# A two-layer hybrid encoder trunk: softmax division after the product with v, and head pairs prepared one step earlier

## The chip, the cores and the metric

The kernel runs on one core of a Trainium2 chip. The time is the device time of one execution, in microseconds; for the kernel before it is 1597.09 us, the median of three runs (1595.65 to 1597.92).

## The reference

Two layers over one sequence of 512 tokens with 1024 features, in float32. Each layer has a mixing part and a feed-forward part.

```python
h = modulate(rms_norm(x, norm_mix[i]), sh1, sc1)      # sh1.. g2 = c_act @ w_ada[i] + b_ada[i], six vectors of 1024
# hybrid_mixer: one projection of h is split among three mixers
o_ssm = s5_mixer(u, ...)                               # 16 groups of a diagonal state-space recurrence
o_mla = block_sweep(q, k, v_mla, ..., chunk_causal)    # 6 heads, low-rank q and kv, rotary part
o_fox = block_sweep(fqh, fkh, fvh, ..., frame_causal, log_decay=cum_log_f)   # 6 heads, forgetting bias
x = x + g1 * (concat(rms_norm of each) @ w_out)
h = modulate(rms_norm(x, norm_ffn[i]), sh2, sc2)
x = x + g2 * (swiglu(h) if i == 0 else moe_ffn(h))     # dense in layer 0, top 2 of 8 experts in layer 1

# block_sweep: 128-query blocks, each reads the keys up to its end
s = einsum(q[q0:q1], k[:q1]) * scale (+ log_decay terms), masked
p = softmax(s);  out = p @ v[:q1]
```

## The kernel before

Features lie on partitions and tokens on the free axis for most stages. A weight block is loaded by the sync engine's DMA queue (`wload`, L375), rounded by ScalarE to its high half (L382) and reduced by VectorE to its low half (L383); each product of the large matrices is then three matmuls (L399 to L401).

**Attention.** The twelve heads of a layer go in six pairs: F0, F1, F2 (the forgetting heads) and M0, M1, M2 (the low-rank heads). A pair is first prepared, by `fox_unit` or `mla_unit`: projections into PSUM, norms of q and k, and four transposes per token block into the tile `U` (three buffers), which ScalarE copies out of PSUM (L961). The low-rank units start with the matmuls L1012 and L1014 in the PSUM banks `C` (two of them); all the units' transposes (`turn`) use the banks `C` as well, and so does `mla_low`, which comes before them. `attend` then does the pair: for each head and each 128-query block i, `att_prob` computes the scores in a bank `A` (L866) and adds the mask (L867), VectorE takes the row maximum (L870), ScalarE the exponential with its row sum (L871), VectorE the reciprocal of the sum (L872), and GpSimd or VectorE multiplies the row block by it (L873). One block later `att_out` transposes the i+1 blocks of 128x128 (L882), ScalarE copies them out (L885), and they go one by one into products with v (L887): 10 products of 128 columns per head, each of which is two instructions in float32. A head writes 64 of the 128 partitions of the output bank, and the two heads of a pair come one after the other. At the pair's end ScalarE copies the bank out (L890).

**What else runs there.** The state-space mixer's parts (`s5_part`, whose products at L821 write the two halves of the partitions by turns); `s5_out`; the merges (three norms over a mixer's output); and the output projection `w`, whose tile `xs` has the buffers of the attention rows `pr`. In layer 0 there are also the rows of the modulation vectors (`ada_part`): one row is a 512 KB DMA into a tile with one buffer and a multiply-and-sum of 1.2 us on VectorE (L477); 40 rows belong to layer 0, row by row, and 24 of them lie in this stage: rows 16 to 24 give g1 for the output projection, 26 to 39 give the shift and scale that the feed-forward norm needs (L527, L516).

**What sets the order.** The string `SEQ` lists the steps of each layer: `f` and `m` prepare a unit, `A` attends the oldest prepared one, `s` is a part of the state-space mixer, `o` its output, `a,j0,j1` are modulation rows, `g` a merge, `w` a block of the output projection. The framework plans every engine's instructions from it, the earlier step first where two are ready, so steps overlap; each engine then runs its own list in order. The rows of a step `a` carry one more edge: on VectorE they come behind the last instruction of the unit prepared last ahead of them in `SEQ` (`held`, with `self.mark` set at L982 and L1045).

Of the kernel before, what the change touches and what calls it, by code (L numbers as in the profile page):

```python
# [53 lines left out]
def _most_blocks():  # L54
# [49 lines left out]
SEQ = ("""k,BBAD v,BD f,0,B p,0,4,1 f,1,A p,4,4,0 R l s,0 A s,1 m,0 A a,16,25 s,2 f,2,C A s,3 a,25,26 A o m,1 A m,2 a,26,34 g,F,A g,5,D a,34,40 A w,0,C g,M,A w,1,C w,2,C w,3,C w,4,C w,5,A w,6,C w,7,D""",
       """k,AACC R f,0,B s,0 s,1 v,A l f,1,C s,2 m,0 A A f,2,B s,3 A m,1 A o m,2 A g,F,C g,5,C A g,M,B w,0,A w,1,C w,2,B w,3,C w,4,C w,5,C w,6,C w,7,C""")
# [180 lines left out]
class Net:  # L286
# [538 lines left out]
    def s5_out(self, l, yj, pool):  # L825

        nc = self.nc
        v = nc.vector
        TT = v.tensor_tensor
        wg = pool.tile([P, 2, 256], FT, tag="sA", name="wg", bufs=1)  # L830
        nc.gpsimd.dma_start(out=wg, in_=self.a["wglu"][l].rearrange("p (k m) -> p k m", k=2))
        yT = pool.tile([P, 2, L], FT, tag="yT", name="yT", bufs=1)
        for th in range(2):
            ps = self.bank("D")
            for t in range(4):
                nc.tensor.transpose(ps[:, t * P:(t + 1) * P], yj[:, th * 4 + t].rearrange("p q c -> p (q c)"),
                                    self.C("ident"))
            for g in range(2):
                nc.scalar.copy(
                    yT[:, g].rearrange("p (j t) -> p t j", t=T8)[:, th * 4:th * 4 + 4, :],  # L840
                    ps.rearrange("p (t g j) -> p t g j", t=4, g=2)[:, :, g, :])

        gt = pool.tile([P, 2, L], FT, tag="yj", name="gt", bufs=1)
        nc.scalar.activation(gt, yT, AF.Square, scale=math.sqrt(0.044715))
        v.scalar_tensor_tensor(out=gt, in0=gt, scalar=1.0, in1=yT, op0=OP.add, op1=OP.mult)
        self.sigmoid(gt, 2.0 * math.sqrt(2.0 / math.pi))
        TT(out=yT, in0=yT, in1=gt, op=OP.mult)
        oT = pool.tile([P, 2, L], FT, tag="o5", name="o5", bufs=1)
        for m in range(2):
            ps = self.bank("D")  # L850
            for k in range(2):
                nc.tensor.matmul(ps, wg[:, k, m * P:(m + 1) * P], yT[:, k], start=(k == 0), stop=(k == 1))
            nc.scalar.activation(oT[:, m], ps, AF.Identity, bias=self.S(l, "bglu")[:, m:m + 1])
        self.sigmoid(oT, 1.0)
        TT(out=oT, in0=oT, in1=yT, op=OP.mult)
        self.dump(f"ossm{l}", oT)
        return oT

    def att_prob(self, un, hh, i, pool):

        nc, sp = self.nc, self.sp
# [4 lines left out]
        nc.tensor.matmul(ps[:, :n], U[0:r, 2 + hh, i * P:n], U[0:r, hh, 0:n], start=True, stop=False)  # L866
        nc.tensor.matmul(ps[:, n - P:n], self.identB, self.mskB[:, un["mask"]], start=False, stop=True)  # L867
        ms = sp.tile([P, 2], FT, tag="ms", name="ms")
        pr = pool.tile([P, L], FT, tag="pr", name="pr", bufs=NPR)
        v.reduce_max(out=ms[:, 0:1], in_=ps[:, :n], axis=AX.X, negate=True)  # L870
        nc.scalar.activation(pr[:, :n], ps[:, :n], AF.Exp, bias=ms[:, 0:1], accum_out=ms[:, 1:2])  # L871
        v.reciprocal(ms[:, 1:2], ms[:, 1:2])  # L872
        (nc.gpsimd if (hh * NT + i) % 8 in PRP else v).tensor_scalar(pr[:, :n], pr[:, :n], ms[:, 1:2], None, op0=OP.mult)  # L873
        return pr

    def att_out(self, un, hh, i, pr, po, pool, oT):

        nc = self.nc
        ps = self.bank("B")
        n = (i + 1) * P  # L880
        for j in range(i + 1):
            nc.tensor.transpose(ps[:, j * P:(j + 1) * P], pr[:, j * P:(j + 1) * P], self.C("ident"))  # L882
        PT = pool.tile([P, L], FT, tag="PT", name="PT", bufs=NPT)
        eng = nc.scalar.copy if (hh * NT + i) % 8 in PTA else nc.vector.tensor_copy
        eng(PT[:, :n], ps[:, :n])  # L885
        for j in range(i + 1):
            nc.tensor.matmul(po[hh * 64:hh * 64 + 64, i * P:n], un["v"][:, j, un["vo"] + hh, :],  # L887
                             PT[:, j * P:(j + 1) * P], start=(j == 0), stop=(j == i))
# [100 lines left out]
    def mla_unit(self, l, u, c, keep, pool, far):  # L989
        nc, sp = self.nc, self.sp  # L990
        v = nc.vector
        TT = v.tensor_tensor
        U = keep.tile([P, 4, L], FT, tag="U", name="U", bufs=NU)
# [14 lines left out]
        for i in range(NT):  # L1008
            tk = slice(i * P, (i + 1) * P)
            ps = self.bank("C")  # L1010
            for k in range(2):
                nc.tensor.matmul(ps[:, :192], cT[:, k, tk], wq[:, k], start=(k == 0),  # L1012
                                 stop=(k == 1))
# [3 lines left out]
                                 scale=rkv[:, i:i + 1])  # L1017
# [16 lines left out]
        qb = far.tile([P, NT, 2, 32], FT, tag="qb", name="qb", bufs=1)  # L1034
# [43 lines left out]
    def mla_low(self, l, h, kf, pool, far):  # L1078

        nc, a = self.nc, self.a  # L1080
        v = nc.vector
        TT = v.tensor_tensor
# [36 lines left out]
        kr2 = far.tile([P, NT, 32], FT, tag="kr2", name="kr2", bufs=1)  # L1119
# [21 lines left out]
    def layer_mix(self, l, xsrc, x, xst):  # L1141

        nc, tc, a = self.nc, self.tc, self.a
        v = nc.vector
        with ExitStack() as st:
            e = st.enter_context
            big = e(tc.tile_pool(name=f"big{l}", bufs=2))
            h = [big.tile([P, KD, L], FR, tag="big", name=f"h{i}") for i in range(2)]
            st3 = e(ExitStack())
            ps = self.norm_sum(x, (0, 2, 4, 6)) if l == 0 else None  # L1150
# [755 lines left out]
```

## Time and profile before

| | |
|---|---|
| profiled execution | 1599.44 us, span 1597.8 us, granted TensorE clock 0.962 |
| busy TensorE, weight loads | 1488.4 us (93%), 1236.8 us (77%) |
| busy VectorE, ScalarE, GpSimd | 1127.7 us (71%), 799.3 us (50%), 207.5 us (13%) |
| attention of layer 0 | about 98 to 300 us of the span, its output projection to 350 us, feed-forward from 357 us |
| attention of layer 1 | about 795 to 966 us |

Times are microseconds from the start of the span. A busy time of TensorE includes matmuls that only overlap in its pipeline, so 93% isn't 93% of its peak. A row of a group ends, after the bar, with the idle time of the engine just before its instructions and what ended it; a row of a timeline gives start, duration and, in brackets, idle time before it and its releaser.

### The profile page before, as it was taken

The numbers are of one execution on the slowest core, as the hardware profiler recorded it, in microseconds if no ns is written. First come the engines' busy times: TensorE is split into PE (matmuls) and PEld (weight loads), VectorE is DVE, ScalarE is ACT, GpSimd is POOL, SyncE is SP. The second block draws the span as 40 slices with busy tenths as digits, with TensorE's granted clock in tenths as the row PEclk, the third lists the DMA queues.
The fourth block names the chain that finished last, engine by engine and source line by source line (L and its number), as shares of the span: only waits on it lengthen the run. The fifth ranks groups of instructions, "written<-read, shape, count | busy, mean of one in ns | idle before, by whom it ended". The sixth has DMA issues, their size and how long they took to land.

```text
span 1597.8 us, 24585 instructions
## 1 busy us (share of the span) xinstructions
PE 1488.4 (93%) x8427; PEld 1236.8 (77%) x8427; DVE 1127.7 (71%) x2636; ACT 799.3 (50%) x1547; POOL 207.5 (13%) x286
## 2 busy tenths in 40 slices
PE   6889899889999999999999999679999999999896
PEld 5877666558888888887988666578878998898894
DVE  8695678866855577555555665778777878878885
ACT  4344357544332233233445863357556766776672
POOL 1213131102000000003322220110000001002002
PEclk7988989999999999999999999789999999999998
DMA  9323440584566657552431006378777878889885
GB/s 357 138 92 123 118 139 34 178 301 132 188 200 191 219 180 230 178 181 82 148 93 54 1 8 201 102 257 284 248 264 284 293 250 306 314 265 319 293 296 190
DMA packets 94722, 308.88 MB, mean 193 GB/s; under 512 B 12144, under 2 KB 12592, under 8 KB 94592
## 3 DMA queue, kind: packets, MB, share of 16 engines
q1 hardware_dynamic: 74880, 253.42, 46.8%
q0 software_dynamic: 12800, 41.26, 7.7%
q10 hardware_dynamic: 6912, 12.59, 2.4%
q8 instruction: 68, 1.11, 0.3%
q14 instruction: 62, 0.51, 0.1%
HBM read 283.43 MB, written 23.79 MB: 192 GB/s over the span
## 4 chain that ended last, share of the span: by engine, by line
PE 62%; DMA 12%; DVE 10%; issue 10%; ACT 3%; POOL 2%; ACTq 0%; DVEq 0%; SPq 0%; POOLq 0%
PE psB L400 4%; PE psB L401 4%; PE psB L399 4%; PE psC L400 4%; PE psC L401 4%; PE psC L399 4%; PE psB L887 3%; DMA adw<-in_wada_dram 3%; PE psA L399 3%; PE psA L401 3%; PE psA L400 3%; PE psA L866 3%; PE psB L1424 2%; PE psB L882 2%; DVE wl L383 2%
## 5 line engine op out<-in xcount | busy, mean ns | idle before, releaser
L382 ACT CAST wh<-wr 128x1024 fp32r<-128x1024 f32 (+4 forms) x402 | 395.3, 992 | 422.8 <-PE psB L400 98.3
L383 DVE TENSOR_TENSOR wl<-wr,wh 128x1024 fp32r<-128x1024 f32 (+4 forms) x402 | 458.5, 1149 | 153.0 <-ACT wh L382 149.0
L477 DVE SCALAR_TENSOR_TENSOR adw<-adw,cact 128x1024 f32<-128x1024 f32 x80 | 97.8, 1223 | 80.1 <-DMA adw<-in_wada_dram 79.9
L866 PE MATMUL psA<-U 65*128 65x128 f32 (+3 forms) x192 | 73.8, 472 | 9.8 <-DVE xn L980 7.6
L1424 PE MATMUL psB<-hgB,wh 128*128 128x432 f32 (+3 forms) x256 | 80.3, 323 | 0.5 <-ACT wh L382 0.5
L870 DVE TENSOR_REDUCE ms<-psA 128x1 f32<-128x128 f32 (+1 forms) x96 | 46.5, 487 | 42.3 <-PE psA L867 41.8
L1426 PE MATMUL psB<-hgB,wl 128*128 128x256 f32 x256 | 71.2, 283 | 0.9 <-DVE wl L383 0.9
L873 POOL TENSOR_SCALAR pr<-pr,ms 128x128 f32<-128x128 f32 (+1 forms) x48 | 49.1, 1024 | 148.6 <-DVE ms L872 100.6
L399 PE MATMUL psB<-fh,wh 128*128 128x512 f32 (+1 forms) x156 | 61.2, 392 | 4.7 <-ACT fh L517 4.7
L1424 PE MATMUL psC<-hgB,wh 128*128 128x432 f32 (+3 forms) x192 | 61.2, 324 | 2.2 <-ACT wh L382 2.0
L400 PE MATMUL psB<-fh,wh 128*128 128x512 f32 (+1 forms) x156 | 61.0, 391 | 1.0 <-POOL fh L520 0.6
L885 ACT COPY PT<-psB 128x128 f32<-128x128 f32 (+1 forms) x96 | 41.4, 436 | 38.7 <-PE psB L882 38.4
L401 PE MATMUL psB<-fh,wl 128*128 128x512 f32 (+1 forms) x156 | 60.6, 388 | 0.0
L1504 POOL DMA_DIRECT2D yd<-yt x21 | 11.8, 563 | 375.4 <-ACT yt L1494 265.7
L871 ACT ACTIVATE pr<-psA,ms 128x128 f32<-128x128 f32 (+1 forms) x96 | 51.6, 539 | 17.2 <-DVE ms L870 14.2
L1424 PE MATMUL psA<-hgB,wh 128*128 128x432 f32 (+3 forms) x184 | 58.7, 325 | 0.1
L1426 PE MATMUL psC<-hgB,wl 128*128 128x256 f32 x192 | 54.0, 284 | 2.7 <-DVE wl L383 2.7
L1426 PE MATMUL psA<-hgB,wl 128*128 128x256 f32 x184 | 51.8, 283 | 0.0
L1424 PEld LDWEIGHTS psB<-hgB,wh 128*128 128x128 f32 x256 | 48.3, 189 | 2.5 <-ACT wh L382 1.7
L1426 PEld LDWEIGHTS psB<-hgB,wl 128*128 128x128 f32 x256 | 48.3, 189 | 1.7 <-DVE wl L383 1.2
L866 PEld LDWEIGHTS psA<-U 65*128 65x128 f32 (+1 forms) x192 | 31.8, 204 | 17.5 <-issue 11.6
L882 PE MATMUL psB<-cst,pr 128*128 128x128 f32 x240 | 43.8, 292 | 0.5 <-POOL pr L873 0.5
(766 smaller groups left out, 4394.8 us busy)
## 6 DMA issues: line engine op xcount, KB each, us to landing
wr<-in_mw_dram SPq DMA_DIRECT2D x158, 512.0 KB, 4.6
adw<-in_wada_dram SPq DMA_DIRECT2D x80, 512.0 KB, 3.7
wr<-in_md_dram SPq DMA_DIRECT2D x80, 512.0 KB, 4.4
wr<-in_fg_dram SPq DMA_DIRECT2D x22, 512.0 KB, 4.3
wr<-in_fu_dram SPq DMA_DIRECT2D x22, 512.0 KB, 4.1
wr<-in_me_dram SPq DMA_DIRECT2D x16, 512.0 KB, 4.4
wr<-in_w_f_dram SPq DMA_DIRECT2D x12, 512.0 KB, 3.6
wr<-in_fd_dram SPq DMA_DIRECT2D x16, 384.0 KB, 3.2
```

The lines of the kernel that those rows point to most:

```text
L382: nc.scalar.copy(hi[:, :n], raw[:, :n])
L383: nc.vector.tensor_tensor(out=lo[:, :n], in0=raw[:, :n], in1=hi[:, :n], op=OP.subtract)
L399: mm(ps, a[0], b[0], start=start, stop=False, skip_group_check=shared)
L400: mm(ps, a[0], b[1], start=False, stop=False, skip_group_check=shared)
L401: mm(ps, a[1], b[0], start=False, stop=stop, skip_group_check=shared)
L477: nc.vector.scalar_tensor_tensor(out=w, in0=w, scalar=1.0, in1=self.cact, op0=OP.mult, op1=OP.mult, accum_out=self.ada[l][:, j:j + 1])
L866: nc.tensor.matmul(ps[:, :n], U[0:r, 2 + hh, i * P:n], U[0:r, hh, 0:n], start=True, stop=False)
L871: nc.scalar.activation(pr[:, :n], ps[:, :n], AF.Exp, bias=ms[:, 0:1], accum_out=ms[:, 1:2])
L873: (nc.gpsimd if (hh * NT + i) % 8 in PRP else v).tensor_scalar(pr[:, :n], pr[:, :n], ms[:, 1:2], None, op0=OP.mult)
L882: nc.tensor.transpose(ps[:, j * P:(j + 1) * P], pr[:, j * P:(j + 1) * P], self.C("ident"))
L1424: mm(ps[:, :2 * C], hi[:, s], h2, start=(kk == 0), stop=False, skip_group_check=True)
L1426: mm(ps[:, C:C + 2 * P], lo[:, s], h2[:, 0:2 * P], start=False, stop=(kk == KD - 1), skip_group_check=True)
```

## The change

The softmax rows are no longer divided before they are transposed. The row sums of both heads are kept, one reciprocal of the 128x8 sums is taken at the pair's end, and small products spread it over the 64 partitions of each head; VectorE multiplies the pair's output by it as it takes it out of PSUM. A head's ten 128x128 blocks are handled in three parts (`TQ`) of 3, 3 and 4 blocks instead of four; the transposed blocks of a whole head are kept (`PT0`, `PT1`), and the products with v come at the pair's end, four per head of 512, 384, 256 and 128 columns, with the two heads by turns. In `SEQ` both layers prepare a unit one attention earlier; the rows `a,16,25` of layer 0 move from behind `m,0` to behind `m,2`; in layer 1 the projection of F2 moves from the banks `B` to `C`. Some tiles change place: `xs` takes the buffers of the state-space parts, `qb`, `kr2` and the spread sums take the common 2 KB tiles, and `yT` becomes two tiles.

```diff
-SEQ = ("""k,BBAD v,BD f,0,B p,0,4,1 f,1,A p,4,4,0 R l s,0 A s,1 m,0 A a,16,25 s,2 f,2,C A s,3 a,25,26 A o m,1 A m,2 a,26,34 g,F,A g,5,D a,34,40 A w,0,C g,M,A w,1,C ...""",
-       """k,AACC R f,0,B s,0 s,1 v,A l f,1,C s,2 m,0 A A f,2,B s,3 A m,1 A o m,2 A g,F,C g,5,C A g,M,B w,0,A ...""")
+SEQ = ("""k,BBAD v,BD f,0,B p,0,4,1 f,1,A p,4,4,0 R l m,0 A s,0 f,2,C A s,1 m,1 A s,2 m,2 a,16,25 A s,3 a,25,26 A o a,26,34 g,F,A g,5,D a,34,40 A w,0,C g,M,A w,1,C ...""",
+       """k,AACC R f,0,B s,0 s,1 v,A l f,1,C s,2 m,0 A f,2,C A s,3 m,1 A m,2 A o A g,F,C g,5,C A g,M,B w,0,A ...""")
+TQ = (((0, 0), (1, 1), (0, 1)), ((2, 2), (0, 2), (1, 2)), ((0, 3), (2, 3), (3, 3), (1, 3)))
+PTO = ((0, 2), (1, 4), (3, 4), (8, 1))
...
-        v.reciprocal(ms[:, 1:2], ms[:, 1:2])
-        (nc.gpsimd if (hh * NT + i) % 8 in PRP else v).tensor_scalar(pr[:, :n], pr[:, :n], ms[:, 1:2], None, op0=OP.mult)
...
+    def att_turn(self, t, pr, at, PT):
+        ps = self.bank("B")
+        for c, (j, i) in enumerate(TQ[t]):
+            o = at[i] + j * P
+            nc.tensor.transpose(ps[:, c * P:(c + 1) * P], pr[:, o:o + P], self.C("ident"))
+        nc.scalar.copy(PT[:, o:o + n], ps[:, :n * P].rearrange("p (a b) -> p a b", a=n))
+
+    def att_out(self, un, PTs, ls, pool, oT):
+        v.reciprocal(ls, ls)
+        ps = self.bank("B")
+        for i in range(NT):
+            for hh in range(2):
+                nc.tensor.matmul(ps[hh * 64:hh * 64 + 64, i * P:(i + 1) * P],
+                                 ls[:, hh, i:i + 1].to_broadcast([P, HD]), self.C("ident"), start=True, stop=True)
+        rl = pool.tile([P, L], FT, tag="t2k", name="rl")
+        nc.scalar.copy(rl, ps)
+        po = self.bank("B")
+        for j in range(NT):
+            o, d = PTO[j]
+            for hh, PT in ((1, PTs[1]), (0, PTs[0])):
+                nc.tensor.matmul(po[hh * 64:hh * 64 + 64, j * P:], un["v"][:, j, un["vo"] + hh, :],
+                                 PT[:, o:o + (NT - 1 - j) * d + 1:d], start=(j == 0), stop=(j == NT - 1),
+                                 skip_group_check=True)
+        v.tensor_tensor(out=oT[:, un["u"], :], in0=po, in1=rl, op=OP.mult)
...
-                    xt = pool.tile([P, L], FT, tag="pr", name="xs", bufs=NPR)
+                    xt = env["far"].tile([P, L], FT, tag="s" + "ABC"[d % 3], name="xs", bufs=1)
```

## Rows read from the trace of the kernel before

**Rows 1.** The page: chain of work that ended last, shares of the span by engine.
```profile
PE 62%; DMA 12%; DVE 10%; issue 10%; ACT 3%; POOL 2%; ACTq 0%; DVEq 0%; SPq 0%; POOLq 0%
```

**Rows 2.** Matmuls, layer 0: start, us, engine, line, operation, tiles, shape, count.
```profile
226.24 0.44 PE L821 MATMUL psD<-sA,sX 128*64 128x128 f32 x4
...
227.16 0.39 PE L821 MATMUL psD<-sB,sU 128*64 128x128 f32 x4
227.39 1.04 PE L887 MATMUL psB<-PT,vm 128*64 128x128 f32 x8
228.35 0.33 PE L882 MATMUL psB<-cst,pr 128*128 128x128 f32 x1
228.52 1.02 PE L866 MATMUL psA<-U 65*128 65x512 f32 x2
229.38 0.22 PE L867 MATMUL psA<-mskB,identB 128*128 128x128 bf16 x1
```

**Rows 3.** Groups by line, layer 1 (756 to 985 us): busy, mean ns | idle.
```profile
L873 POOL TENSOR_SCALAR pr<-pr,ms 128x128 f32<-128x128 f32 (+1 forms) x24 | 24.6, 1023 | 72.1 <-DVE ms L872 49.5 <-DVE uss L1025 10.5 <-DVE kq L1043 7.1
...
L873 DVE TENSOR_SCALAR pr<-pr,ms 128x256 f32<-128x256 f32 (+1 forms) x24 | 10.2, 424 | 1.2
...
L872 DVE RECIPROCAL ms<-ms 128x1 f32<-128x1 f32 x48 | 7.6, 159 | 12.6 <-ACT pr L871 12.3
```

**Rows 4.** ScalarE's timeline, layer 1: the pair outputs of F1 and M2.
```profile
884.03 0.58 ACT L890 COPY oF<-psB 128x512 f32<-128x512 f32 x1
...
965.73 0.59 ACT L890 COPY oM<-psB 128x512 f32<-128x512 f32 x1 [2.05 <-PE psB L887]
```

**Rows 5.** VectorE's timeline, layer 0: modulation rows and units' last instructions.
```profile
177.24 1.22 DVE L477 SCALAR_TENSOR_TENSOR adw<-adw,cact 128x1024 f32<-128x1024 f32 x1
...
183.04 1.23 DVE L477 SCALAR_TENSOR_TENSOR adw<-adw,cact 128x1024 f32<-128x1024 f32 x1 [3.04 <-DMA adw<-in_wada_dram]
...
225.19 1.22 DVE L477 SCALAR_TENSOR_TENSOR adw<-adw,cact 128x1024 f32<-128x1024 f32 x1
...
267.75 0.62 DVE L1045 TENSOR_TENSOR kq<-qr,urr 128x192 f32<-128x192 f32 x2
268.29 1.22 DVE L477 SCALAR_TENSOR_TENSOR adw<-adw,cact 128x1024 f32<-128x1024 f32 x1
...
298.55 1.23 DVE L477 SCALAR_TENSOR_TENSOR adw<-adw,cact 128x1024 f32<-128x1024 f32 x1 [0.42 <-DMA adw<-in_wada_dram]
```

**Rows 6.** VectorE's timeline, later: last modulation rows, output projection, feed-forward norm.
```profile
309.83 1.22 DVE L477 SCALAR_TENSOR_TENSOR adw<-adw,cact 128x1024 f32<-128x1024 f32 x1
...
319.94 0.75 DVE L1243 SCALAR_TENSOR_TENSOR xs<-psC,ada,xs 128x512 f32<-128x512 f32 x1 [0.62 <-PE psC L401]
...
350.40 1.22 DVE L477 SCALAR_TENSOR_TENSOR adw<-adw,cact 128x1024 f32<-128x1024 f32 x1
...
356.18 0.88 DVE L516 SCALAR_TENSOR_TENSOR nt<-x,nA,nr 128x256 f32<-128x256 f32 x2
```

**Rows 7.** TensorE's timeline: the first product of the feed-forward part.
```profile
357.25 0.58 PE L399 MATMUL psB<-fh,wh 128*128 128x256 f32 x1 [3.87 <-ACT fh L517]
```

**Rows 8.** Stretches: us, busy PE, PEld, DVE, ACT, POOL, granted clock, DMA share, GB/s.
```profile
300.00:352.00 52.00, 46.96 (x182) 34.47 (x183) 39.30 (x61) 20.44 (x35) 4.28 (x9) 0.97 0.85 289
352.00:372.00 20.00, 14.30 (x64) 10.62 (x63) 17.65 (x30) 10.46 (x17) 6.82 (x4) 0.83 0.34 115
```

**Rows 9.** TensorE's timeline, layer 0: first matmuls of units M0 and M2.
```profile
157.78 0.92 PE L1012 MATMUL psC<-wq,cT 128*128 128x192 f32 x4
...
249.90 0.59 PE L1012 MATMUL psC<-wq,cT 128*128 128x192 f32 x2
```

**Rows 10.** ScalarE's timeline, layer 0: last copies into U of M0, F2, M1.
```profile
184.87 0.57 ACT L961 COPY U<-psC 96x512 f32<-96x512 f32 x1
...
225.93 0.57 ACT L961 COPY U<-psC 65x512 f32<-65x512 f32 x1
...
248.52 0.57 ACT L961 COPY U<-psC 96x512 f32<-96x512 f32 x1
```

More of the change, by code (lines that the diff above doesn't have):

```diff
@@ L96 @@
 ADP = 2
-PRP = (0, 2, 4, 6)
 NVU = P + 38 + 256
@@ L103 @@
 FIRST = (("w_vu", NVU, FSD), ("w_f0", 256, "B"))
[L104 to L105 removed]
+SEQ = ("""k,BBAD v,BD f,0,B p,0,4,1 f,1,A p,4,4,0 R l m,0 A s,0 f,2,C A s,1 m,1 A s,2 m,2 a,16,25 A s,3 a,25,26 A o a,26,34 g,F,A g,5,D a,34,40 A w,0,C g,M,A w,1,C w,2,C w,3,C w,4,C w,5,A w,6,C w,7,D""",
+       """k,AACC R f,0,B s,0 s,1 v,A l f,1,C s,2 m,0 A f,2,C A s,3 m,1 A m,2 A o A g,F,C g,5,C A g,M,B w,0,A w,1,C w,2,B w,3,C w,4,C w,5,C w,6,C w,7,C""")
 ADN = (2, 2)
@@ L831, in s5_out @@
         nc.gpsimd.dma_start(out=wg, in_=self.a["wglu"][l].rearrange("p (k m) -> p k m", k=2))
-        yT = pool.tile([P, 2, L], FT, tag="yT", name="yT", bufs=1)
+        yT = [pool.tile([P, L], FT, tag=f"s{n}", name=f"yT{n}", bufs=1) for n in "BC"]
         for th in range(2):
@@ L839, in s5_out @@
                 nc.scalar.copy(
-                    yT[:, g].rearrange("p (j t) -> p t j", t=T8)[:, th * 4:th * 4 + 4, :],
+                    yT[g].rearrange("p (j t) -> p t j", t=T8)[:, th * 4:th * 4 + 4, :],
                     ps.rearrange("p (t g j) -> p t g j", t=4, g=2)[:, :, g, :])
         gt = pool.tile([P, 2, L], FT, tag="yj", name="gt", bufs=1)
-        nc.scalar.activation(gt, yT, AF.Square, scale=math.sqrt(0.044715))
-        v.scalar_tensor_tensor(out=gt, in0=gt, scalar=1.0, in1=yT, op0=OP.add, op1=OP.mult)
+        for g in range(2):
+            nc.scalar.activation(gt[:, g], yT[g], AF.Square, scale=math.sqrt(0.044715))
+            v.scalar_tensor_tensor(out=gt[:, g], in0=gt[:, g], scalar=1.0, in1=yT[g], op0=OP.add, op1=OP.mult)
         self.sigmoid(gt, 2.0 * math.sqrt(2.0 / math.pi))
-        TT(out=yT, in0=yT, in1=gt, op=OP.mult)
+        for g in range(2):
+            TT(out=yT[g], in0=yT[g], in1=gt[:, g], op=OP.mult)
         oT = pool.tile([P, 2, L], FT, tag="o5", name="o5", bufs=1)
@@ L851, in s5_out, with att_prob @@
             for k in range(2):
-                nc.tensor.matmul(ps, wg[:, k, m * P:(m + 1) * P], yT[:, k], start=(k == 0), stop=(k == 1))
+                nc.tensor.matmul(ps, wg[:, k, m * P:(m + 1) * P], yT[k], start=(k == 0), stop=(k == 1))
             nc.scalar.activation(oT[:, m], ps, AF.Identity, bias=self.S(l, "bglu")[:, m:m + 1])
         self.sigmoid(oT, 1.0)
-        TT(out=oT, in0=oT, in1=yT, op=OP.mult)
+        for g in range(2):
+            TT(out=oT[:, g], in0=oT[:, g], in1=yT[g], op=OP.mult)
         self.dump(f"ossm{l}", oT)
         return oT
-    def att_prob(self, un, hh, i, pool):
+    def att_prob(self, un, hh, t, ls, pool):
         nc, sp = self.nc, self.sp
@@ L863, in att_prob @@
         ps = self.bank("A")
-        n = (i + 1) * P
+        pr = pool.tile([P, L], FT, tag="pr", name="pr", bufs=NPR)
+        ms = sp.tile([P, 2], FT, tag="ms", name="ms")
         U, r = un["U"], un["rows"]
[L866 to L869, printed above, removed]
@@ L870, in att_prob @@
-        v.reduce_max(out=ms[:, 0:1], in_=ps[:, :n], axis=AX.X, negate=True)
-        nc.scalar.activation(pr[:, :n], ps[:, :n], AF.Exp, bias=ms[:, 0:1], accum_out=ms[:, 1:2])
-        v.reciprocal(ms[:, 1:2], ms[:, 1:2])
-        (nc.gpsimd if (hh * NT + i) % 8 in PRP else v).tensor_scalar(pr[:, :n], pr[:, :n], ms[:, 1:2], None, op0=OP.mult)
-        return pr
-    def att_out(self, un, hh, i, pr, po, pool, oT):
+        at = {}
+        o = 0
+        for i in sorted({i for _, i in TQ[t]}):
+            n = (i + 1) * P
+            at[i] = o
+            s = slice(o, o + n)
+            nc.tensor.matmul(ps[:, s], U[0:r, 2 + hh, i * P:n], U[0:r, hh, 0:n], start=True, stop=False)
+            nc.tensor.matmul(ps[:, o + n - P:o + n], self.identB, self.mskB[:, un["mask"]], start=False, stop=True)
+            m = ms[:, len(at) - 1:len(at)]
+            v.reduce_max(out=m, in_=ps[:, s], axis=AX.X, negate=True)
+            nc.scalar.activation(pr[:, s], ps[:, s], AF.Exp, bias=m, accum_out=ls[:, hh, i:i + 1])
+            o += n
@@ L878, in att_out @@
+        return pr, at
+    def att_turn(self, t, pr, at, PT):
         nc = self.nc
         ps = self.bank("B")
[L880 to L888, printed above, removed]
@@ L889, in att_out @@
-        if hh == 1 and i == NT - 1:
-            nc.scalar.copy(oT[:, un["u"], :], po)
+        for c, (j, i) in enumerate(TQ[t]):
+            o = at[i] + j * P
+            nc.tensor.transpose(ps[:, c * P:(c + 1) * P], pr[:, o:o + P], self.C("ident"))
+        n = len(TQ[t])
+        o = sum(len(x) for x in TQ[:t])
+        nc.scalar.copy(PT[:, o:o + n], ps[:, :n * P].rearrange("p (a b) -> p a b", a=n))
+    def att_out(self, un, PTs, ls, pool, oT):
+        nc = self.nc
+        v = nc.vector
+        v.reciprocal(ls, ls)
[14 more added lines that the diff above has]
+        v.tensor_tensor(out=oT[:, un["u"], :], in0=po, in1=rl, op=OP.mult)
@@ L892, in attend @@
     def attend(self, un, pool, oT):
-        po = None
+        PTs = []
+        ls = self.sp.tile([P, 2, NT], FT, tag="ls", name="ls", bufs=2)
         for hh in range(2):
-            for i in range(NT):
-                pr = self.att_prob(un, hh, i, pool)
+            for t in range(len(TQ)):
+                pr, at = self.att_prob(un, hh, t, ls, pool)
                 self.att_end(ADP)
-                if po is None:
-                    po = self.bank("B")
-                self.pend.append(lambda hh=hh, i=i, pr=pr, po=po: self.att_out(un, hh, i, pr, po, pool, oT))
+                if t == 0:
+                    PTs.append(pool.tile([P, 10, P], FT, tag=f"PT{hh}", name=f"PT{hh}", bufs=1))
+                self.pend.append(lambda t=t, pr=pr, at=at, PT=PTs[hh]: self.att_turn(t, pr, at, PT))
@@ L903, in att_end, with end @@
+        last = self.pend.pop()
+        def end():
+            last()
+            self.att_out(un, PTs, ls, pool, oT)
+        self.pend.append(end)
     def att_end(self, left=1):
@@ L1118, in mla_low @@
         kro = far.tile([P, NT, 32], FT, tag="kro", name="kro", bufs=1)
-        kr2 = far.tile([P, NT, 32], FT, tag="kr2", name="kr2", bufs=1)
+        kr2 = pool.tile([P, L], FT, tag="t2k", name="kr2")[:, :P].rearrange("p (i e) -> p i e", i=NT)
         kr = kf[:, :, 0:32]
```

4 lines of the change are left out of this document (1 added, 3 removed).

## The prediction

> **What bounds the kernel now.** I read the chain that ended last first: 62% of the span hangs on TensorE, 12% on DMA, 10% on VectorE [rows 1]. The change touches the mixing parts of both layers, so I went on to those stretches alone. In layer 1 there are no modulation rows; the pairs' outputs follow each other from F1 at 884.03 to M2 at 965.73 us, four pairs in 81.7 us, 20.4 us each [rows 4], and TensorE is the engine that runs through. So there a cheaper pair shortens the stage. In layer 0 two chains end nearly together. One is x: attention, output projection, norm. The other is the modulation rows: the last one starts at 350.40 and takes 1.22 us, and its scale is needed by the first norm instruction at 356.18, after which the feed-forward's first product runs at 357.25 [rows 6, 7]. That is 4.6 us of slack. The reader should see in [rows 5] what starts these rows: 0.1 us or less after the last instruction of the unit ahead of them (L1045, two instructions in 0.62 us from 267.75), the first row runs at 268.29, though its data had long been loaded; ten rows were done before, 177.24 to 225.19, behind M0 in the same way.
>
> **The pair itself.** Before, a pair issues 40 instructions of 128 columns for the products with v. Eight of them take 0.96 us to the start of the next other matmul [rows 2], which at 0.11 each leaves 0.08 for the change to another kind. Per pair that is 40 x 0.11 + 8 x 0.08 = 5.0 us. After, there are 16 instructions: two each of 512, 384, 256 and 128 columns per head. The scores show 0.43 us per instruction of 512 columns (228.52 to 229.38, two) [rows 2], so one head's eight take 2 x 0.43 x 1280/512 = 2.15 us, both 4.3. Whether the halves overlap is shown at L821, which writes the two halves by turns: 20 instructions in 226.24 to 227.55, 0.27 us of which is the last one's own pipeline, so about 0.05 each against 0.11 [rows 2]. I take overlap, which leaves the first instruction alone: 2.15 + 0.43 = 2.6 us. The new products that spread the sums are 16 instructions of 128 columns by turns: 0.9 us. With two changes of kind the pair costs 3.7, so 1.3 us less; without overlap it costs 4.3 + 1.75 + 0.16 = 6.2, 1.2 us more. Six pairs per layer: -8 us of TensorE time, bound +7.
>
> VectorE loses 8 reciprocals of 0.159 and 4 divisions of 0.424 per pair and gains one reciprocal of 0.16 and one multiply out of PSUM (0.75, by the row of L1243): -2.1 us [rows 3, 6]. GpSimd loses 4 divisions of 1.02 us [rows 3]. ScalarE has six copies out of PSUM instead of eight, and one copy of the spread sums for the one of the output (0.58) [rows 4]: between 0 and -1 us, no more than cover. Each step loses the reciprocal and the division from its chain, on average 0.16 + 0.72 us, and TensorE waits a little less often. The new tail of a pair (2.6 us of products, 0.75 us of VectorE) lies beside the next pair's scores, except after M2, where the output projection covers it; uncovered it costs 3 us less the 0.9 + 0.58 that it replaces, 2 us.
>
> For layer 1 I take -8 from TensorE and -3 from shorter chains and fuller preparation: -11 us. The bounds are +7 (no overlap) and -18, if each of six pairs drops from 20.4 to 17.4 us because nothing but TensorE limits it.
>
> **Layer 0, the order.** Ten modulation rows move from behind M0 to behind M2, so all 24 now follow one mark. The mark before is at 268.3. The 14 rows behind it took 268.29 to 351.62, 83.3 us. With 24 rows the chain needs ten more intervals; a row costs 5.04 us where DMA is free (six intervals, 268.29 to 298.55), 5.33 in the first batch (nine, 177.24 to 225.19), and 8.1 from 309.83 to 350.40 (five) [rows 5, 6], where DMA is 85% busy over the stretch [rows 8]. So the mark must come some 46 us earlier, by 222, or this chain ends later than before.
>
> How early can it come? Units use the banks C in the order of `SEQ`, and that order is unchanged: M0, F2, M1, M2. Before, M0 runs 157.78 to 185.4 (27.7 us), F2 to 226.5 (41), M1 to 249.1 (22.6), and M2's first matmul is at 249.90, its mark 18.4 us later [rows 5, 9, 10]. What goes: F2 lost VectorE to modulation rows: eight of them at 1.3 us and idle waits such as the 3.04 at 183.04 [rows 5], so 41 becomes about 22, the length of M1, which had no rows beside it. M0 loses the state-space part ahead of it and a row: 27.7 to 22. M1 and M2's start shrink little: 22 and 17. M0 may start 2 us earlier, as F0's divisions leave VectorE. So the mark comes at 155.5 + 22 + 22 + 22 + 17 = 238 (estimate). Bounds: 228 with 20, 18, 20 and 15; 258 with nothing gained but the rows (157.8 + 27.7 + 30 + 24 + 18.4).
>
> From 238: nine rows at 5.2 to 285, four at 8.1 while the output projection loads (the first three `xs` loads come earlier, so I take four, not five), eleven at 4.8, a little under the 5.04 as DMA is then alone. Together 132 us, so the last row ends at 370, and the first feed-forward product comes 1.5 us later, at 371.5 instead of 357.25: +14 us. The x chain doesn't set this end: its attention is 8 us cheaper and less often starved, g1 is there at 285, and its projection needs the 50 us it needed before, so x ends near 330. The rows before 238 that VectorE no longer waits for are thus a gain without effect; what is late next is the row chain. The other moved tiles (`xs`, `qb`, `kr2`, `yT`) I cost at 0: the first `xs` loads only come sooner, the others have idle buffers, and if one waits it is for a transfer of a few us under TensorE's work.
>
> One rule is weighed here. In the stretch of the feed-forward's start, 352 to 372, the granted clock is 0.83, a mix of 1.2 and 2.4 GHz, after TensorE had waited 3.87 us [rows 7, 8]. The Trainium skill ("TensorE: Matmul & The Clock Gate", Part 1) says that the throttled clock is the default and that activity releases it. By the row the low clock there is paid already, 17% of 20 us, 3.4 us; by the rule a start after some 40 us of idle TensorE stays low longer, and the sum would be up to 3 us higher. I take +1.
>
> **Sum.** +14 +1 -11 = +4 on the profiled execution's 1599.4 us (span 1597.8 and 1.6 around it), 1603.4. That execution lies 2.35 us over the median of the runs, so I state 1601.0.
>
> **Rivals.**
> 1. The row chain isn't late. Units run faster without rows beside them, the mark comes at 228, and rows run at 5.04 all through: the last ends at 349, the first product near 351, -6 us; with layer 1 at -12 the time is 1579. For it: the units' shares of VectorE shrink most just there. Against: the 8.1 us rows. It decides from a mark by about 232, or row intervals under 5.1. This is the other side: faster.
> 2. The banks C stay the chain in both layers. In layer 1 F2's projection now comes into that chain (it lay in B), so M2's unit isn't ready earlier, and that layer gains 3 at most; in layer 0 the units need 24, 26, 24 and 18, the mark comes at 247.5, and the first product at 382: +25 -3 = 1619.
> 3. The halves don't overlap with long columns: +1.2 instead of -1.3 us per pair. Layer 0 keeps +14 as the rows set its end, layer 1 is at -11 + 15 = +4 less the shorter chains: +14 to +18 in all, 1613. Against it stands L821, which overlaps with shared and with separate right sides; for it, that no row shows it beyond 128 columns.
>
> **Chances.** The forecast has 0.48, with a range of its own of 1588 to 1616 (mark 232 to 246, layer 1 -15 to -6); rival 1 has 0.30, rival 2 0.14, rival 3 0.08. The range that leaves out no more than two in ten is 1580 to 1621. A change of 0.2% (3.2 us) is about what a measurement of this kernel can tell from none. Faster: 0.27 of rival 1 and 0.06 of the forecast, 0.33. Within: 0.11 of the forecast, 0.03 of rival 1, 0.01 of rival 3, 0.15. Slower: 0.52.
>
> **What would show it.** In the trace after: the long products of L887's successor at about 0.43 us for two instructions of different halves (overlap) or for one (rival 3). VectorE's first L477 behind the mark at 238, the last ending at 370, and TensorE idle ahead of the first feed-forward product; a last row by 352 shows rival 1. M2's output in layer 1 at 955 less layer 0's shift if the pair got cheaper; if M2's copies into U come no earlier than before relative to M0's, rival 2. The forecast is wrong if the feed-forward starts at 357 or earlier, or if layer 1's mixing part shortens by less than 4 us.

## The result: 1.3% slower, and the profile after

The changed kernel takes 1616.89 us (median of four runs, 1609.57 to 1621.97) against 1596.37 us for the kernel before; the ratio is 1.0133, with a 95% interval of 1.0094 to 1.0171. The forecast was 1601.0 us, with a range of 1580 to 1621. The profiled execution took 1609.57 us (span 1607.9), 10.1 over the one of before; it is the shortest of the four, so its trace holds half of the loss of the medians.

The chain that ended last, by engine and by line (its first part), as in [rows 1]: DMA gains a point, and the modulation rows' DMA, 3% of the chain before, leads the lines now.

```profile
PE 61%; DMA 13%; DVE 10%; issue 10%; ACT 4%; POOL 1%; ACTq 0%; SPq 0%; DVEq 0%; POOLq 0%
DMA adw<-in_wada_dram 5%; PE psC L402 5%; PE psC L401 5%; PE psC L400 5%; PE psB L401 4%; PE psB L400 4%; PE psB L402 4%; PE psA L402 3%; PE psA L400 3%; PE psA L401 3%; DMA wr<-in_mw_dram 2%; DVE wl L384 2%; PE psA L877 2%; DVE adw L478 2%; PE psB L1461 2%
```

VectorE's timeline of layer 0, which answers to [rows 5, 6]: L1082 is the unit's last instruction (the mark), L478 a modulation row, L517 the first norm instruction of the feed-forward part.

```profile
241.63 0.61 DVE L1082 TENSOR_TENSOR kq<-qr,urr 128x192 f32<-128x192 f32 x2
242.16 1.21 DVE L478 SCALAR_TENSOR_TENSOR adw<-adw,cact 128x1024 f32<-128x1024 f32 x1
...
246.81 1.23 DVE L478 SCALAR_TENSOR_TENSOR adw<-adw,cact 128x1024 f32<-128x1024 f32 x1 [0.24 <-DMA adw<-in_wada_dram]
...
368.21 1.23 DVE L478 SCALAR_TENSOR_TENSOR adw<-adw,cact 128x1024 f32<-128x1024 f32 x1 [3.31 <-DMA adw<-in_wada_dram]
...
372.83 1.22 DVE L478 SCALAR_TENSOR_TENSOR adw<-adw,cact 128x1024 f32<-128x1024 f32 x1 [3.39 <-DMA adw<-in_wada_dram]
...
374.50 1.28 DVE L517 SCALAR_TENSOR_TENSOR nt<-x,nA,nr 128x256 f32<-128x256 f32 x3
```

All 24 rows stand behind one mark, the last two wait for their own DMA, and the norm follows. TensorE's timeline beside it (against [rows 7]): after the sums of the norm it has nothing for 35.33 us, then the feed-forward starts at 375.58 instead of 357.25.

```profile
337.41 2.84 PE L498 MATMUL psA<-sq,ones 128*128 128x512 f32 x6 [0.79 <-DVE sq L495]
375.58 0.58 PE L400 MATMUL psB<-fh,wh 128*128 128x256 f32 x1 [35.33 <-ACT fh L518]
```

The stretches there (columns as in [rows 8]): the idle one has a granted clock of 0.58, nearly the lower level of 1.2 GHz, and the 20 us behind it 0.78, where before had 0.83.

```profile
340.00:374.00 34.00, 0.26 (x1) 0.00 (x0) 11.68 (x23) 1.78 (x4) 0.00 (x0) 0.58 0.37 127
374.00:394.00 20.00, 18.17 (x81) 15.42 (x82) 15.26 (x25) 8.70 (x13) 7.17 (x4) 0.78 0.31 105
```

The pair's end in layer 1, TensorE's timeline, against [rows 2]: sums spread (L906), products with v (L915), next work. Then VectorE's last multiply of M2, against the output in [rows 4].

```profile
968.85 1.09 PE L906 MATMUL psB<-cst,ls 128*64 128x128 f32 x16
969.77 2.32 PE L915 MATMUL psB<-PT,vm 128*64 128x512 f32 x16
972.02 0.50 PE L400 MATMUL psA<-mg,wh 128*128 128x512 f32 x1
```

```profile
972.22 0.69 DVE L918 TENSOR_TENSOR oM<-psB,rl 128x512 f32<-128x512 f32 x1 [0.83 <-PE psB L915]
```

Layer 1's first norm instruction is at 755.49, and was at 738.75 before (VectorE's timeline, after and before):

```profile
755.49 0.87 DVE L517 SCALAR_TENSOR_TENSOR nt<-x,nA,nr 128x256 f32<-128x256 f32 x2
```

```profile
738.75 0.87 DVE L516 SCALAR_TENSOR_TENSOR nt<-x,nA,nr 128x256 f32<-128x256 f32 x2
```

M2's output follows 216.7 us later, before 227.0: in these two executions the pairs gained 10.3 us. But behind M2 there is a loss. ScalarE's DMA queue, layer 1 (L1281 stores a block of `xs`, L1300 reloads it as `x`; issues), after:

```profile
998.89 0.33 ACTq L1281 DMA_DIRECT2D xs<-xs  x1
1001.38 3.71 ACTq L1300 DMA_DIRECT2D x<-xs  x8
1005.18 0.83 ACT L383 CAST wh<-wr 128x768 fp32r<-128x768 f32 x1 [6.42 <-DMA x<-xs]
```

and before (L1244 and L1263), where the reloads lay between the stores:

```profile
980.72 0.33 ACTq L1263 DMA_DIRECT2D x<-xs  x1
982.69 0.33 ACTq L1236 DMA_DIRECT2D xs<-xd  x1
983.11 0.39 ACTq L1244 DMA_DIRECT2D xs<-xs  x1
983.53 2.08 ACTq L1263 DMA_DIRECT2D x<-xs  x3
...
999.83 0.33 ACTq L1263 DMA_DIRECT2D x<-xs  x1
```

VectorE's additions into x show who waits, after, and TensorE's router products behind them:

```profile
1004.29 0.75 DVE L1309 SCALAR_TENSOR_TENSOR x<-psA,ada,x 128x512 f32<-128x512 f32 x1 [2.63 <-DMA x<-xs]
...
1006.09 0.74 DVE L1309 SCALAR_TENSOR_TENSOR x<-psB,ada,x 128x512 f32<-128x512 f32 x1
...
1017.85 0.75 DVE L1309 SCALAR_TENSOR_TENSOR x<-psC,ada,x 128x512 f32<-128x512 f32 x1 [0.33 <-PE psC L402]
...
1032.32 0.75 DVE L1309 SCALAR_TENSOR_TENSOR x<-psA,ada,x 128x512 f32<-128x512 f32 x1 [1.30 <-PE psA L402]
```

```profile
1006.22 2.53 PE L1565 MATMUL psC<-ws,ones 128*128 128x8 f32 x16 [4.08 <-DVE ws L1561]
```

From M2's output to the last of these additions it is 60.1 us, before 54.0 (965.73 to 1019.69, the last addition of before):

```profile
1019.69 0.75 DVE L1272 SCALAR_TENSOR_TENSOR x<-psA,ada,x 128x512 f32<-128x512 f32 x1 [1.29 <-PE psA L401]
```

So the profiled 10.1 us are five terms: +18.3 to the start of layer 0's feed-forward, -1.6 from there to layer 1 (382.6 to 381.0), -10.3 in layer 1's pairs, +6.1 behind them, and -2.5 from there to the end (578.1 to 575.6), where the code is the same.

### The profile page after: what moved, and what is told of

Same layout as the page of the kernel before. It is cut to its first block, busy times and chain, and to the rows that moved or that the text cites. A ratio compares the mean times of both kernels' runs of the same rounds, so it can differ in the third digit from the quotient of the medians.

```text
span 1607.9 us, 24059 instructions
## 1 busy us (share of the span) xinstructions
PE 1461.5 (91%) x8331; PEld 1214.6 (76%) x8331; DVE 1108.1 (69%) x2522; ACT 795.0 (49%) x1525; POOL 155.2 (10%) x238
## 4 chain that ended last, share of the span: by engine, by line
PE 61%; DMA 13%; DVE 10%; issue 10%; ACT 4%; POOL 1%; ACTq 0%; SPq 0%; DVEq 0%; POOLq 0%
DMA adw<-in_wada_dram 5%; PE psC L402 5%; PE psC L401 5%; PE psC L400 5%; PE psB L401 4%; PE psB L400 4%; PE psB L402 4%; PE psA L402 3%; PE psA L400 3%; PE psA L401 3%; DMA wr<-in_mw_dram 2%; DVE wl L384 2%; PE psA L877 2%; DVE adw L478 2%; PE psB L1461 2%
## 5 line engine op out<-in xcount | busy, mean ns | idle before, releaser
L478 DVE SCALAR_TENSOR_TENSOR adw<-adw,cact 128x1024 f32<-128x1024 f32 x80 | 97.8, 1223 | 100.6 <-DMA adw<-in_wada_dram 100.6
L877 PE MATMUL psA<-U 65*128 65x128 f32 (+5 forms) x192 | 71.4, 458 | 10.2 <-DVE xn L1017 7.6
L880 DVE TENSOR_REDUCE ms<-psA 128x1 f32<-128x128 f32 (+2 forms) x96 | 45.7, 485 | 37.4 <-PE psA L878 36.9
L400 PEld LDWEIGHTS psB<-fh,wh 128*128 128x128 f32 x156 | 30.0, 192 | 41.8 <-ACT fh L518 36.2
L881 ACT ACTIVATE pr<-psA,ms 128x128 f32<-128x128 f32 (+2 forms) x96 | 51.1, 535 | 11.9 <-DVE ms L880 11.5
L894 ACT COPY PT<-psB 128x384 f32<-128x384 f32 (+1 forms) x72 | 37.2, 523 | 22.6 <-PE psB L891 22.0
L891 PEld LDWEIGHTS psB<-cst,pr 128*128 128x128 f32 x240 | 27.0, 143 | 25.5 <-ACT pr L881 7.1
## 6 DMA issues: line engine op xcount, KB each, us to landing
wr<-in_fd_dram SPq DMA_DIRECT2D x16, 384.0 KB, 3.1
```

Source lines behind the costliest of these rows:

```text
L400: mm(ps, a[0], b[0], start=start, stop=False, skip_group_check=shared)
L478: nc.vector.scalar_tensor_tensor(out=w, in0=w, scalar=1.0, in1=self.cact, op0=OP.mult, op1=OP.mult, accum_out=self.ada[l][:, j:j + 1])
L877: nc.tensor.matmul(ps[:, s], U[0:r, 2 + hh, i * P:n], U[0:r, hh, 0:n], start=True, stop=False)
L880: v.reduce_max(out=m, in_=ps[:, s], axis=AX.X, negate=True)
L881: nc.scalar.activation(pr[:, s], ps[:, s], AF.Exp, bias=m, accum_out=ls[:, hh, i:i + 1])
L891: nc.tensor.transpose(ps[:, c * P:(c + 1) * P], pr[:, o:o + P], self.C("ident"))
```

## Experiments

Theory: two separate things cost, the rows behind M2's mark and the place of `xs`, and without them the new pair makes the kernel faster. Rivals are named with each run. A ratio is against the kernel before, with its 95% interval.

**Ten rows back behind M0.**

```diff
-... m,0 A s,0 f,2,C A s,1 m,1 A s,2 m,2 a,16,25 A s,3 ...
+... m,0 A s,0 a,16,25 f,2,C A s,1 m,1 A s,2 m,2 A s,3 ...
```

> The changed kernel with one edit: ten of the modulation rows of layer 0 stand again right behind M0 in the order of work, the other fourteen behind M2. Theory (the chain of rows behind M2's mark sets the end of layer 0): with ten intervals of about 4.6 us gone from behind the mark, the rows end near 330 us and the first feed-forward product runs at 340 to 350 us instead of 375.6; the whole time is 25 to 35 us below the changed kernel's, 1585 to 1592 us. Rival (the rows are late because VectorE is full, not because of their place): the rows beside F2 and M1 push the mark of M2 back by 13 us or more, the first product stays within 8 us of 375.6, and the time is within 8 us of the changed kernel's. The end of layer 1 is as in the changed kernel under both: all eight reloads of x issued at once, after the last store of xs.

1596.24 us, ratio 0.9988 (0.9969 to 1.0008): 20.6 us below the changed kernel. VectorE's last modulation row and first addition into x, then TensorE's first feed-forward product:

```profile
326.83 1.23 DVE L478 SCALAR_TENSOR_TENSOR adw<-adw,cact 128x1024 f32<-128x1024 f32 x1 [2.78 <-DMA adw<-in_wada_dram]
...
337.46 0.75 DVE L1309 SCALAR_TENSOR_TENSOR x<-psA,ada,x 128x512 f32<-128x512 f32 x1 [6.43 <-DMA x<-xs]
```

```profile
356.73 0.38 PE L400 MATMUL psB<-fh,wh 128*128 128x256 f32 x1 [3.87 <-ACT fh L518]
```

The rows end 28 us before the product, so they aren't its bound any more, and the mark of M2 moves from 242 to 248 only: the rival falls. But the product came 7 us later than the theory's latest, and the time lies 4 above its range: x is late now. Its first addition ran here at 337.46 and waited 6.43 us for `x<-xs`; next come `xs` and then both.

**`xs` back in the mixing part's pool.**

```diff
-xt = env["far"].tile([P, L], FT, tag="s" + "ABC"[d % 3], name="xs", bufs=1)
+xt = pool.tile([P, L], FT, tag="pr", name="xs", bufs=NPR)
```

> The changed kernel with one edit: the tile xs of the output projection is taken from the mixing part's pool again, as before the change, instead of from the pool of the buffers sA, sB and sC. Theory (the new place of xs holds back the reload of x, as the x tile reuses that pool's memory): in layer 1 the reloads of x are issued between the stores of xs again, the first about 18 us ahead of the last instead of all within 1 us, the wait of TensorE of some 4 us at the router's products goes, and the time is 6 to 11 us below the changed kernel's; layer 0 stays as it is, since its rows are later than x. Rival (the reloads are late because of the order of the transfers in their queue): the reloads stay together and the time within 3 us.

1608.28 us, ratio 1.0074 (1.0047 to 1.0100): 8.6 us below the changed kernel. The size is loose: the changed kernel's interval (1.0094 to 1.0171) touches this one, and the profiled execution, 1611.64 us at a mean granted clock of 0.951, is no shorter than the changed kernel's at 0.957. The reloads in ScalarE's queue lie between the stores again:

```profile
999.38 0.91 ACTq L1300 DMA_DIRECT2D x<-xs  x2
1000.33 0.44 ACTq L1281 DMA_DIRECT2D xs<-xs  x1
...
1000.89 1.30 ACTq L1300 DMA_DIRECT2D x<-xs  x2
1002.29 0.67 ACTq L1281 DMA_DIRECT2D xs<-xs  x1
...
1016.61 0.33 ACTq L1300 DMA_DIRECT2D x<-xs  x1
```

From M2's output to the last addition it is 54.7 us instead of 60.1. So the place of `xs` decides, not the order in the queue, which is the same code. Why the place does is an inference from the code: the x tile takes over the memory of the closed pool of `sA`, `sB` and `sC`, so it must wait for the last store out of it. The changed kernel's trace fits: its first reload is issued 2.5 us after the last store (998.89 to 1001.38), and a store of `xs` there takes 2.0 us or more to land. No run took the two pools' memory apart.

**Both edits.**

> The changed kernel with both edits: ten rows back behind M0, and xs back in the mixing part's pool. Theory (two separate causes): their gains add up, 31 to 46 us below the changed kernel's time, 1572 to 1586 us, which is 10 to 24 us faster than the kernel before: what the cheaper pairs give in layers 0 and 1 is then left over. Rival (the pairs themselves give nothing, and layer 1's attention only looks shorter): within 5 us of the kernel before.

1579.83 us (1577.69 to 1582.67), ratio 0.9896 (0.9867 to 0.9926): 37 us below the changed kernel and 16.5 below the kernel before. The two causes add, and more than add: `xs` is worth 8.6 us with the rows late and 16.4 with the rows early, because only then its wait in layer 0 is uncovered. In the profiled executions of this run and of the one with the rows alone, the way from M2's output to the first feed-forward product is 59.7 instead of 68.1 us, and in layer 1 from M2's output to the last addition 54.4 instead of 60.4: 14.5 of the 16.4. Another 5.5 us of layer 0 lie ahead of M2's output, where nothing waits for x yet; there the granted clock in 130 to 135 us was 1.00 here and 0.50 in the other. The first feed-forward product:

```profile
342.85 0.58 PE L400 MATMUL psB<-fh,wh 128*128 128x256 f32 x1 [3.87 <-ACT fh L518]
```

**The rows alone, in the kernel before.** Its pair and its preparation are kept; only the rows go.

```diff
-... m,0 A a,16,25 s,2 f,2,C A s,3 a,25,26 A o m,1 A m,2 a,26,34 ...
+... m,0 A s,2 f,2,C A s,3 A o m,1 A m,2 a,16,25 a,25,26 a,26,34 ...
```

> The kernel before with one edit: all 24 modulation rows stand behind M2 in the order of work, none behind M0; nothing of the pair's products or of the preparation ahead is changed. Theory (the place of the rows costs by itself): without rows beside F2 the mark of M2 comes at about 255 us instead of 268, and 24 rows in 132 us end near 387 us, so the feed-forward starts about 30 us later and the time is 25 to 35 us over that of before. Rival (the rows' place is harmless, the loss comes from the new preparation or the new pairs): within 5 us of before.

1627.61 us, ratio 1.0195 (1.0152 to 1.0237), 31 us over before. VectorE's first row and the norm behind the last one, then TensorE's first product:

```profile
253.30 1.22 DVE L477 SCALAR_TENSOR_TENSOR adw<-adw,cact 128x1024 f32<-128x1024 f32 x1
...
383.13 1.22 DVE L477 SCALAR_TENSOR_TENSOR adw<-adw,cact 128x1024 f32<-128x1024 f32 x1 [3.31 <-DMA adw<-in_wada_dram]
...
384.80 1.28 DVE L516 SCALAR_TENSOR_TENSOR nt<-x,nA,nr 128x256 f32<-128x256 f32 x3
```

```profile
385.88 0.58 PE L399 MATMUL psB<-fh,wh 128*128 128x256 f32 x1 [33.51 <-ACT fh L517]
```

The loss needs neither the new pair nor the preparation: 24 rows behind one mark take 131 us here and 132 in the changed kernel, with the mark 11 us earlier.

**The pair without the preparation.** The changed kernel's code with the order of before in both layers, and `xs` in the mixing part's pool.

```diff
-... R l m,0 A s,0 f,2,C A s,1 m,1 A s,2 m,2 a,16,25 A s,3 a,25,26 A o a,26,34 ...
+... R l s,0 A s,1 m,0 A a,16,25 s,2 f,2,C A s,3 a,25,26 A o m,1 A m,2 a,26,34 ...
-... s,2 m,0 A f,2,C A s,3 m,1 A m,2 A o A g,F,C ...
+... s,2 m,0 A A f,2,B s,3 A m,1 A o m,2 A g,F,C ...
```

> The changed kernel's pair (products with v in long columns by turns, three parts per head, division after them, spread sums) with the order of work of the kernel before in both layers, and xs in the mixing part's pool: the new pair alone. Theory (pairs cost TensorE 3.3 us instead of 5.0 each, and the preparation one step ahead is the smaller part): 8 to 16 us faster than the kernel before, 1580 to 1588 us, and the output of M2 in layer 1 6 to 10 us earlier relative to the start of the layer's norm. Rival (the new pair only pays with the preparation ahead, since without it a step waits for its own unit): within 4 us of the kernel before.

1577.12 us (1570.22 to 1586.11), ratio 0.9905 (0.9872 to 0.9937). M2's output is 213.2 us behind layer 1's first norm instruction, 13.8 less than before, where 6 to 10 were expected. The median lies 3 us under the theory's range, and its claim holds: the pair alone gives the whole gain.

**The preparation without the pair.** The kernel before with the changed order, ten rows behind M0.

> The kernel before with the changed kernel's order of work in both layers, one step of preparation ahead, but ten modulation rows behind M0 as before, and nothing else: the preparation ahead alone. Theory (a step's wait for its own unit is a few us, but the pair's old division leaves TensorE as full as before): 0 to 8 us faster than the kernel before. Rival (the preparation is the whole gain of the version with both repairs): 12 to 18 us faster, as fast as that version. Rival 2 (bank C with F2's projection in it holds the units up): slower by 3 us or more.

1602.13 us, ratio 1.0056 (1.0035 to 1.0078), 7 us slower. In its profiled execution layer 1 is within 2 us (M2's output 225.4 behind the norm), and layer 0's first feed-forward product comes at 363.12, 5.9 later. But that execution is the shortest of the six, 1596.30 us, 3 less than the profiled one of the kernel before, so it doesn't hold the loss of the medians. The rival that the preparation is the gain falls; the theory's sign was wrong too. Rival 2 named the sign, but the units didn't come later: M2's last copy into `U` is at 267.3, before 275.6. What the 5.9 us in layer 0 are isn't settled, nor where the 7 lie.

**The two heads not by turns.** The version with both edits, the loops over heads and blocks exchanged in L906 and L915.

```diff
-for j in range(NT):
-    for hh, PT in ((1, PTs[1]), (0, PTs[0])):
+for hh, PT in ((1, PTs[1]), (0, PTs[0])):
+    for j in range(NT):
```

> The version with both repairs (ten rows behind M0, xs in the mixing part's pool), but the products that spread the sums and those with v are issued head by head instead of by turns of the two heads. Theory (two products into different halves of the columns overlap also with 512 columns, and only by turns): a pair's 16 products with v take 4.3 us instead of 2.3 and the 16 spread sums 1.75 instead of 1.0, 2.7 us per pair more; with 12 pairs, of which those in layer 1 are all on the path, 12 to 30 us slower than the version with both repairs. Rival (products of both heads overlap whichever way they are issued, or the pair's products lie beside other waits): gaps as by turns, or the time within 4 us.

1593.90 us, ratio 0.9997 (0.9979 to 1.0015): 14 us over the version by turns, and no different from before. TensorE's timeline, layer 1:

```profile
955.16 1.58 PE L906 MATMUL psB<-cst,ls 128*64 128x128 f32 x16
956.57 3.88 PE L914 MATMUL psB<-PT,vm 128*64 128x512 f32 x16
960.38 0.50 PE L400 MATMUL psA<-mg,wh 128*128 128x512 f32 x1
```

By turns the two took 1.0 and 2.3 us to the next kind, here 1.4 and 3.8, so 2.0 us per pair (2.7 was expected). On TensorE the pair then costs 5.2 us, no less than the 5.0 that [rows 2] give for before. M2's output is 226.7 us behind the norm, as before the change; by turns it was 223.6 in the profiled execution of the version with both edits and 215.8 to 219.0 in the four others with that pair and order in layer 1. In the medians the gain is gone without the turns: in this version it is the overlap of the two halves.

**F2's projection in bank B, layer 1.** The version with both edits, and this in layer 1:

```diff
-... s,2 m,0 A f,2,C A s,3 ...
+... s,2 m,0 A f,2,B A s,3 ...
```

> The version with both repairs, but in layer 1 the projection of F2 uses bank B, as before the change, instead of bank C. Theory (bank C isn't the chain in layer 1): within 3 us of the version with both repairs. Rival (the second rival of the prediction: bank C is the chain, and F2's projection in it delays the unit of F2): 4 us or more faster.

1585.26 us, ratio 0.9940 (0.9917 to 0.9962): 5.4 us over, outside the theory's 3, and not the rival's gain. M2's output is at 219.1, inside the 215.8 to 223.6 of the five executions with bank C, so nothing shows that the bank holds layer 1. The profiled executions of the two take the same time (1577.6 and 1577.7 us), so no trace shows a cause for the 5.4, and the two intervals overlap (0.9867 to 0.9926 with both edits alone).

**One layer each in the order of before.** The version with both edits, with layer 1 in the old order, and then with layer 0.

> The version with both repairs, but layer 1 is in the order of the kernel before (each pair prepared right ahead of its own step); layer 0 keeps the preparation one step ahead. Theory (in layer 1 the new pair alone gives the gain, and the preparation ahead costs some 3 us of it): M2's output 213 to 215 us behind the start of the layer's first norm instruction, against 216 to 224 with the preparation ahead; the time 0 to 5 us below the version with both repairs, 1574 to 1580 us. Rival (the preparation ahead gives 3 us in layer 1, as the prediction had it): 3 us or more over the version with both repairs.

> The version with both repairs, but layer 0 is in the order of the kernel before, rows included; layer 1 keeps the preparation one step ahead. Theory (with ten rows behind M0 the preparation ahead neither gives nor costs in layer 0): first feed-forward norm instruction at 340 to 345 us, the time within 4 us of the version with both repairs, 1576 to 1584 us. Rival (preparation ahead pays in layer 0, where the pairs wait more): 346 us or later, 5 us or more over the version with both repairs.

Layer 1 old: 1585.16 us, ratio 0.9939 (0.9913 to 0.9964), M2's output at 220.5, not 213 to 215. The theory, drawn from the one trace of the pair without the preparation, missed, and the number is the rival's. The stretch 800 to 850 of the two executions, which have the same order in layer 1, shows what set that trace apart (without the preparation; then layer 1 old):

```profile
800.00:850.00 50.00, 48.05 (x385) 40.16 (x385) 30.49 (x107) 27.07 (x75) 8.19 (x20) 1.00 0.19 58
```

```profile
800.00:850.00 50.00, 46.84 (x351) 37.40 (x350) 26.82 (x91) 25.22 (x69) 10.46 (x22) 0.90 0.23 72
```

A granted clock of 0.90 instead of 1.00 goes with 7 us in that layer. Layer 0 old: 1577.16 us, ratio 0.9884 (0.9856 to 0.9912), first norm instruction at 342.8: as expected. It is the fastest ratio, 1.2% below before, though its interval overlaps with two others. With the new pair the preparation moves the time by a few us at most, and these intervals don't settle its sign in either layer.

## Why the prediction was right, and where it failed

**The rows (+14): right in place and mechanism, too short.** The forecast had the mark at 238, 24 rows in 132 us and the last ending at 370. Measured: first row at 242.16, 24 rows in 131.9 us, last end near 374, first product 18.3 us later than before. The chain's length held; the units' times, from which its start was worked out, didn't. M0, F2, M1 and M2 (to its mark) took 24.0, 27.6, 22.7 and 19.2 us, 93.5 in all, where 22, 22, 22 and 17 were taken; most of the miss is F2, which was said to fall to the length of M1 once no rows lay beside it. M0 began at 148.70, 7 us ahead of the forecast, and that hid more than half of the miss. It was luck of this execution: TensorE's granted clock over 100 to 150 us was 0.97, against 0.86 in the profiled execution of the kernel before. In the run with `xs` alone put back it was 0.84; there M0 began at 156.32, the units took the same 93.6 us, the first row ran at 249.93, and the first product came at 384.02, 26.8 us later than before. x was ready near 340, not 330, without effect.

**The clock ahead of the feed-forward (+1): nothing.** The granted clock was 0.78 behind a 35 us pause, 0.83 before behind 3.87, so the row moved the way the rule of the Trainium skill ("TensorE: Matmul & The Clock Gate", Part 1) says. Over the 20 us from the first product on, the two are closer: 0.82 and 0.85. And from there to layer 1 took 1.6 us less than before, so neither the +1 nor the rule's +3 is to be seen.

**The pair in layer 1 (-11): -10.3 in this execution.** The four other profiled executions with the same pair and order in layer 1 gained 3 to 11 us on the 227.0 of before, the least of them at a granted clock of 0.87 in 800 to 850 us. The products with v overlap, 2.3 us for 2.6, sums 1.0 for 0.9, 3.3 for 3.7 in all. The other engines got what the steps said for 12 pairs: VectorE is busy 1108.1 us instead of 1127.7 (-20, -25 forecast), GpSimd 155.2 instead of 207.5 (-52, -49). The -11's parts are less sure than their sum: the run without turns leaves nothing of the gain in the medians, so the -3 for preparation and shorter chains wasn't shown.

**"The other moved tiles I cost at 0": the step that failed.** The argument for `xs` was that its first loads come sooner. They do (in layer 0 at 254.99 instead of 293.91 us), but the reload of x that follows the stores went unlooked at: +6.1 us in layer 1's profile, 8.6 in the medians, and 16.4 once the rows no longer cover layer 0's share. Every DMA of a moved tile counts, those that take over its memory included.

**The size.** +4 was forecast on the profiled execution, +10.1 came: 4.3 by the rows, 6.1 by `xs`, 0.7 by the pairs, less 2.6 and 2.5 by the clock term and the tail. The medians differ by 20.5, and that other half no term covers. The median of 1616.89 lies inside the stated range, but 0.9 us outside the 1588 to 1616 that the forecast had for itself, and nearest to the 1619 of the second rival. So the direction and its cause were forecast; that the range held is in part luck, as it had been widened for rivals.

The four executions stand in the order of their mean granted clocks, 0.957, 0.954, 0.949 and 0.947 for 1609.57, 1615.38, 1618.40 and 1621.97 us; the kernel before ran at 0.960 to 0.970 in the later comparisons. One place is seen in two executions whose code is the same up to there, 130 to 135 us of the changed kernel, then of the run with `xs` alone put back; the third row is the kernel before:

```profile
130.00:135.00 5.00, 4.82 (x42) 3.73 (x41) 4.17 (x20) 3.24 (x10) 0.33 (x1) 1.00 0.14 55
```

```profile
130.00:135.00 5.00, 5.00 (x19) 3.72 (x19) 3.04 (x18) 1.93 (x6) 0.37 (x1) 0.50 0.39 149
```

```profile
130.00:135.00 5.00, 5.00 (x18) 3.21 (x18) 2.01 (x12) 1.64 (x5) 0.79 (x2) 0.50 0.38 146
```

At 0.50, the 1.2 GHz level, 19 matmuls stand in the row instead of 42. The profiled 10.1 us thus set a changed kernel without this stretch against a kernel before that had it; with it the feed-forward starts at 384.0 instead of 375.6. With all rows behind one mark, such a loss ahead of the mark reaches the end in full. That fits the changed kernel's wide spread, 12 us; that it is the whole difference wasn't shown.

**The rivals.** The first (rows not late) needed a mark by 232; it came at 242. The second (banks C) had 3 us of gain at most in layer 1, where four of five executions gained 7.9 or more, and the move to bank B gained nothing. But its times for the units of layer 0 (24, 26, 24 and 18 us, first product +25) came nearer than the forecast's; whether the banks C set those times, no run tested in layer 0. The third (no overlap) is refuted by the products' times.

## What to carry to other kernels

A change that moves a chain of loads behind a later point has to be priced by that chain's own length from its new start: here 24 rows at 5.5 us each gave the length to a microsecond, while the start, worked out from four units, was off by 4 to 12. The gain of the main edit only showed once the rows were put back. When a tile changes its pool, follow what will next live in the memory it gets, and look at that tile's transfers too. Take single executions for where time goes, not for effects of a few us: with the same code in layer 1, two of them differed there by 7, beside granted clocks of 1.00 and 0.90.

## What the runs showed of the hardware

Two float32 matmuls that write different halves of the partitions overlap when issued by turns, with 512 columns as with 128: 16 products with v took 2.3 us by turns and 3.8 head by head. TensorE's granted clock fell to 0.50 in one execution and stayed at 1.00 in another at the same place of the same code, after nearly equal pauses (1.6 and 1.7 us idle in the 10 us from 120).
